# A hybrid decoder layer on one core: weight sums and stores one step later, accumulators loaded ahead, operand jobs on three tiles

## The chip, the cores and the metric

The kernel runs on one core of one Trainium2 chip. The metric is the device time of one execution in microseconds (us), as the median of several runs. The engines are named as in the profile: PE (matmul, with its weight loads PEld), DVE, ACT, POOL, and SP, which here only issues DMAs. Each engine and each engine's DMA queue takes its instructions in a fixed order; an instruction that waits holds up all that stand behind it on the same engine.

## The reference

One layer with 1024 tokens and width 1024. The input is normalised, projected into three branches (M: mLSTM, D: differential attention, C: cross-attention into 256 memory tokens), and each branch's output y is projected again; a sigmoid gate from the same normalised input weighs each projection, and the sum goes through an output projection and back onto the residual. A squared-ReLU MLP of width 4096 follows.

```python
g_m, g_d, g_c = jnp.split(jax.nn.sigmoid(h @ w_gate[l] + b_gate[l]), N_BRANCH, axis=-1)
merged = g_m * (y_m @ w_proj_m[l]) + g_d * (y_d @ w_proj_d[l]) + g_c * (y_c @ w_proj_c[l])
x = x + merged @ w_out[l]
h2 = rms_norm(x, norm_mlp_g[l])
x = x + jnp.square(jax.nn.relu(h2 @ w_up[l])) @ w_down[l]
```

All is float32. A float32 operand is split into a rounded high part (ACT, a cast) and a remainder (DVE, a subtraction), and a product is made of three matmuls (`mm3`, L119).

## The kernel before

**The first part** (to 1250 us on the trace) makes the normalised input `hT`, runs branch C, branch M and branch D, and spreads the gate projections (`gate_steps`, L449, 12 groups of 32 steps, a step is one `mm3` of 3 matmuls) between them. Two runs of gate steps stand by themselves: 64 steps between branch M and branch D (L1672), and 96 steps after branch D (L1695). The branches leave their outputs in DRAM (`yd`), the gates theirs (`gdr`).

**Operand jobs.** The branch projections, the MLP's up and down projection use a scheme with 7 instead of 8 block products (`PROD`, L1123). It needs sums of operand blocks. For an operand x, four blocks are combined by four subtractions (`wino_t`, L1134: three on DVE, one on POOL). For the branch outputs this is done by jobs (`x_jobs`, L1141): a job loads blocks of y on SP, makes the sums, and stores the result to DRAM (`xtd`) on SP. The jobs are a generator that is stepped once for each gate step; `waits` says how many steps lie between load, sums, store and the next load. In the run ahead of branch D there are eight jobs of 512 columns (C 0 to 3, M 3 to 0) on two tiles, after branch D eight of 256 columns (D 0 to 3) on one tile.

**The stream** (`stream`, L1280, from 1252 us to the end) is a row of steps n = 0 to 187: 48 for the branches in the order C, M, D (12 runs of four steps), 12 for the output projection, 64 for the up projection U (16 runs of four, u = 0 to 15), 64 for the down projection N (16 passes p of four). A step of a branch, of U or of N is 21 matmuls of 128x512 into seven PSUM banks (bank names rotate over eight); at the end of a run `sums` (L1335) combines the seven banks on ACT and DVE, and the next run takes over the banks as they come free.

Beside the matmuls of step n stand, in program order, `side(n)` (L1304): first the weight split for step n + 3, then a list `todo[n]` of other work, which `at(n, ...)` fills.

- *Weights.* `self.raws` lists raw weights, mostly in pairs (two steps' worth). `w_load` (L1194) issues a pair's two DMAs on SP into one of two buffers (`wrs`) and right behind them the pair's four sums on POOL (`wino_s`, L1127). `w_split` (L1213) splits one step's weights into one of three buffers (`wos`) with ACT and DVE, and when it has split the last of a pair it calls `w_load` for the next pair that uses that buffer.
- *Operands.* `x_load` (L1232) loads an x operand into one of the slots of `SLOT` on SP, `x_split` (L1248) splits it with ACT and DVE. A slot comes free when PE has used the operand that it held. For M and D, operand 0 is loaded at step 5 and 21, and 1 to 3 at 12 to 14 and 28 to 30. `x_direct` (L1255) makes a U operand from SBUF, with `wino_t`.
- *Gates.* `fetch` (L1309) loads a gate's tiles on SP, `gate` (L1314) multiplies on DVE and adds on POOL, `operands` (L1327) splits the merged sum for the output projection.
- *U's results.* `use_up` (L1491) scales a run's four results and squares them, and stores three blocks to `rd` from ACT's queue; `up_rest` (L1500) makes the four sums with `wino_t` and stores them on SP, at step 64 + 4u (u = 15 at 126). N's operands are loaded from `rd`.
- *Accumulators.* N has four groups g of seven accumulators in SBUF. In the first pass of each group (p = g) four of them are loaded with the residual (`x1d`) on SP when the pass's matmuls are traced, then the banks are added (DVE) or copied (ACT). The accumulators take over the memory of the pools that `accum` closes at step 126, among them the two tiles of `use_up` and `up_rest`.

**What sets the order.** Calls through `self.V`, `self.G`, `self.S`, and in the stream `self.A`, are pinned (`InOrder`, L57): each is kept behind the instruction that was traced just before it on its engine. Calls through `nc.vector`, `nc.sync` and the like are not pinned; the framework places them by its own estimate. Gate steps and their stores, and the sums of jobs, are of this kind; loads and stores of jobs are pinned.

Of the kernel before, what the change touches and what calls it, by code (L numbers as in the profile page):

```python
# [71 lines left out]
class Layer:  # L72
# [1068 lines left out]
    def x_jobs(self, pool, jobs, n, waits):  # L1141

        nc = self.nc
        for s, kp in jobs:
            for c in range(0, 512, n):
                r = pool.tile([P, 4, n], F32, tag="xj", name=self.name("xj"))
                for k in range(2):
                    src = self.yd[self.YOF[s]][2 * kp + k].rearrange("p (h n) -> p h n", h=2)
                    self.S.dma_start(r[:, 2 * k : 2 * k + 2], src[:, :, c : c + n])
                for _ in range(waits[0]):  # L1150
                    yield
                self.wino_t(r, r, nc.vector, nc.gpsimd)
                for _ in range(waits[1]):
                    yield
                self.S.dma_start(self.xtd[s][kp][:, :, c : c + n], r)
                for _ in range(waits[2]):
                    yield

    def s_open(self):
# [31 lines left out]
        self.X, self.W, self.wraw, self.nraw = {}, {}, {}, 0  # L1191
        return right

    def w_load(self):  # L1194
# [12 lines left out]
        else:  # L1207
            for i, s in enumerate(srcs):
                self.S.dma_start(r[:, i, 0:4], s)
            self.wino_s(r, self.G)  # L1210
            self.wraw[m] = [r[:, i] for i in range(2)]

    def w_split(self, m, split=None):  # L1213
# [10 lines left out]
        if i == len(self.wraw[j]) - 1:  # L1224
            self.w_load()

# [27 lines left out]

    def x_direct(self, s, kp, b):  # L1255
# [3 lines left out]
        self.wino_t(b, b, self.V, self.G)  # L1259
        self.split2(t[:, 0, 3:7], t[:, 1, 3:7], b)  # L1260

    def s_early(self):

        self.x_load("C", 0)
        self.w_load()
        yield
        self.x_load("C", 1)
        self.w_load()
        for _ in range(20):
            yield  # L1270
        for kp in range(2):
            for i in range(2):
                self.x_split("C", kp, (i,), self.split)
                for _ in range(10):
                    yield
        for kp in range(2):
            self.w_split(kp, self.split)
            yield

    def stream(self):  # L1280
# [23 lines left out]
        def side(n):  # L1304
            self.w_split(n + 3)
# [73 lines left out]
        self.w_split(2)  # L1379
# [23 lines left out]
        self.w_split(n + 3)  # L1403
# [41 lines left out]
        for g in range(4):  # L1445
# [12 lines left out]
            if g == 3:  # L1458
# [4 lines left out]
                self.w_split(n + 3)  # L1463
# [36 lines left out]
        def up_rest(u):  # L1500
            t = T["o"].tile([P, 4, 512], F32, tag="o", name=self.name("xts"))
            self.wino_t(T["b"], t, V, G)
            S.dma_start(self.rd[u, :, 3:7], t)

        for u in range(16):
            at(126 if u == 15 else 64 + 4 * u + (u == 0), up_rest, u)
# [16 lines left out]

        at(126, accum)
        for u in range(16):
# [3 lines left out]
            self.w_split(n + 3)  # L1529
# [20 lines left out]

# [225 lines left out]
```

## Time and profile before

| | us |
|---|---|
| median of three runs | 2334.99 |
| the runs | 2328.87 to 2336.34 |
| the profiled execution | 2336.45 |
| its span, first to last instruction | 2334.7 |

| engine | busy us of the span | share |
|---|---|---|
| PE | 2171.2 | 93% |
| DVE | 1493.0 | 64% |
| ACT | 1022.1 | 44% |
| POOL | 591.6 | 25% |

The mean granted TensorE clock is 0.969. Times on the trace count from the span's start. In a trace row, `out<-in` gives the tiles by their names in the program: `xj` is a job's tile, `xo` an operand x, `wraw` raw weights, `wo` split weights, `p` a PSUM bank, `u` and `c` results of `sums`, `gl` a gate's tile, `mg` the merged sum, `rq` and `xts` the tiles of `use_up` and `up_rest`, `acc` an accumulator, `dsg`, `dq`, `dk`, `dv` tiles of branch D, `y`, `gates`, `r_d`, `x_d` and `xtC_d` tensors in DRAM. L67 is the line of the pinning helper, so that many rows have that line. A row of SPq is the issue of DMAs, not their transfer.

### The profile page before, as it was taken

The page shows a single profiled execution, that of the slowest core. Times are in us where ns is not written, and L with a number is a line of the kernel's source. Part 1 is how long each engine was busy: PE and PEld are TensorE (multiplying, and loading weights), DVE is VectorE, ACT ScalarE, POOL GpSimd, SP SyncE. Part 2 cuts the span into 40 slices and gives each one's busy share as a digit, 9 for nine tenths or more (in the row PEclk, how much of TensorE's full clock was granted, in tenths as well). Part 3 has the DMA queues.
Part 4 walks back from the last instruction along what each step waited for, and adds up shares of the span by engine and source line. Part 5 has one row for each costly group of instructions (what it writes and reads, how often), then busy time and mean ns, then how long its engine had stood idle before and what let it go on. Part 6 is the DMA issues. An engine that isn't in the chain of part 4 may idle for free.

```text
span 2334.7 us, 30365 instructions
## 1 busy us (share of the span) xinstructions
PE 2171.2 (93%) x10953; PEld 1852.5 (79%) x10953; DVE 1493.0 (64%) x2732; ACT 1022.1 (44%) x1991; POOL 591.6 (25%) x564
## 2 busy tenths in 40 slices
PE   7999999999969999999996998899899997679999
PEld 5788888888869999999875776787688876568887
DVE  6643566553337777777532878874677776446789
ACT  6543445443226666666531333233344444323333
POOL 2100000000111111111011446623444443234542
PEclk9999999999979999999998999999999998789999
DMA  6023222212853333333365455233244445444444
GB/s 237 28 93 107 64 69 77 70 49 72 287 162 88 91 91 91 89 84 80 90 215 178 148 203 198 86 122 131 92 139 152 155 166 212 165 136 148 150 149 162
DMA packets 127676, 299.26 MB, mean 128 GB/s; under 512 B 13569, under 2 KB 30246, under 8 KB 120486
## 3 DMA queue, kind: packets, MB, share of 16 engines
q1 hardware_dynamic: 125222, 284.75, 38.2%
q10 hardware_dynamic: 2304, 12.58, 1.3%
q8 instruction: 86, 1.41, 0.3%
q14 instruction: 64, 0.52, 0.1%
HBM read 196.58 MB, written 75.53 MB: 117 GB/s over the span
## 4 chain that ended last, share of the span: by engine, by line
PE 66%; DMA 11%; DVE 10%; ACT 4%; issue 4%; POOL 3%; SPq 2%; DVEq 0%; POOLq 0%; ACTq 0%
PE mm L93 29%; PE p L93 25%; PE sc L93 5%; DMA xj<-y 4%; PE po L93 3%; DVE wo L67 2%; PE tp L96 2%; SPq L67 1%; POOL wraw L67 1%; DVE u L67 1%; DVE gl L67 1%; DMA acc<-x_d 1%; ACT xo L67 1%; DMA y<-yd 1%; DMA gl<-gates 1%
## 5 line engine op out<-in xcount | busy, mean ns | idle before, releaser
L93 PE MATMUL p<-xo,wo 128*128 128x512 f32 x3696 | 884.1, 401 | 97.1 <-DVE acc L67 24.7
L93 PEld LDWEIGHTS p<-xo,wo 128*128 128x128 f32 x3696 | 709.9, 193 | 270.0 <-DVE acc L67 26.4
L93 PE MATMUL mm<-w,hT 128*128 128x384 f32 (+3 forms) x2496 | 477.4, 334 | 33.9 <-DVE dsg L114 26.3
L67 POOL TENSOR_TENSOR wraw<-wraw 128x256 f32<-128x256 f32 x352 | 370.9, 1064 | 538.8 <-DMA wraw<-in_wdown 198.2
L93 PE MATMUL mm<-hT,w 128*128 128x512 f32 x1920 | 465.9, 395 | 3.1 <-ACT gt L473 3.1
L93 PEld LDWEIGHTS mm<-w,hT 128*128 128x128 f32 x2496 | 392.8, 191 | 48.3 <-issue 21.4
L93 PEld LDWEIGHTS mm<-hT,w 128*128 128x128 f32 x1920 | 353.3, 188 | 77.7 <-ACT gt L473 4.0
L67 ACT CAST wo<-wraw 128x896 fp32r<-128x896 f32 (+1 forms) x186 | 172.4, 932 | 455.3 <-PE p L93 277.1
L67 DVE TENSOR_TENSOR wo<-wraw,wo 128x896 fp32r<-128x896 f32 (+1 forms) x186 | 231.4, 1250 | 149.3 <-ACT wo L67 148.8
L114 DVE TENSOR_TENSOR w<-raw,w 128x256 fp32r<-128x256 f32 (+3 forms) x272 | 129.1, 497 | 58.9 <-ACT w L113 58.3
L113 ACT CAST w<-raw 128x256 fp32r<-128x256 f32 (+3 forms) x272 | 121.0, 469 | 67.6 <-PE mm L93 25.0
L1009 ACT ACTIVATE dpe<-sc,dst,drr 128x256 f32<-128x256 f32 (+7 forms) x128 | 106.7, 834 | 100.0 <-DVE dst L1005 92.6
L67 DVE TENSOR_TENSOR xo<-xo 128x1536 fp32r<-128x1536 f32 (+1 forms) x58 | 124.3, 2153 | 32.7 <-ACT xo L67 32.5
L67 ACT CAST xo<-xo 128x1536 fp32r<-128x1536 f32 (+1 forms) x58 | 97.3, 1691 | 47.3 <-DMA xo<-y 26.1
L129 POOL TENSOR_SCALAR hss<-hss 128x4 f32<-128x4 f32 x8 | 3.3, 411 | 414.6 <-ACT mscr L754 272.7
L1001 DVE CUSTOM_DVE_ANT_0 sc<-sc,tmask 128x256 f32<-128x256 f32 (+7 forms) x128 | 96.9, 757 | 12.6 <-PE sc L93 12.6
L67 DVE TENSOR_TENSOR u<-u,p 128x512 f32<-128x512 f32 x140 | 93.7, 686 | 12.0 <-PE p L93 0.5
L93 PE MATMUL sc<-dk,dq 128*128 128x512 f32 (+3 forms) x384 | 90.4, 343 | 0.0
L129 POOL TENSOR_SCALAR drr<-drr 128x16 f32<-128x16 f32 x16 | 3.3, 206 | 304.1 <-DVE drr L955 304.1
L93 PE MATMUL po<-mh,wo 128*128 128x512 f32 x256 | 78.9, 389 | 0.0
L473 ACT ACTIVATE gt<-mm,dv 128x512 f32<-128x512 f32 x48 | 32.9, 688 | 103.3 <-PE mm L93 55.0
L93 PE MATMUL po<-dv,daT 128*128 128x256 f32 x576 | 75.4, 274 | 0.6 <-DVE daT L114 0.6
(268 smaller groups left out, 2474.6 us busy)
## 6 DMA issues: line engine op xcount, KB each, us to landing
xo<-r_d SPq DMA_DIRECT2D x19, 1024.0 KB, 9.2
dk<-dsg SPq DMA_DIRECT2D x64, 256.0 KB, 4.0
wraw<-in_wup SPq DMA_DIRECT2D x64, 256.0 KB, 4.2
r_d<-xts SPq DMA_DIRECT2D x16, 1024.0 KB, 4.9
wraw<-in_wdown SPq DMA_DIRECT2D x64, 256.0 KB, 3.1
xo<-r_d SPq DMA_DIRECT2D x19, 768.0 KB, 7.2
raw<-in_wgate SPq DMA_DIRECT2D x48, 256.0 KB, 3.2
gates<-gt SPq DMA_DIRECT2D x48, 256.0 KB, 3.3
```

What stands on the lines that cost most here:

```text
L67: return self.tc.keep_in_program_order(f(*a, **k))
L93: self.pin(self.nc.tensor.matmul(out, l, r, start=start, stop=stop))
L96: self.pin(self.nc.tensor.transpose(out, x, self.ident))
L113: nc.scalar.copy(hi, src)
L114: nc.vector.tensor_sub(lo, src, f32(hi))
L129: g.tensor_scalar(r, ss, 1.0 / width, EPS, op0=ALU.mult, op1=ALU.add)
L473: nc.scalar.activation(t, ps, AF.Tanh, bias=self.bg[:, ft : ft + 1], scale=0.5)
L1001: V.tensor_tensor_reduce(out=sc[:, 0:n], in0=sc[:, 0:n], in1=self.tmask[:, D - n : D], scale=1.0, scalar=-3.0e38, op0=ALU.add, op1=ALU.max ...
L1009: nc.scalar.activation(pe[c][:, 0:n], sc[:, 0:n], AF.Exp, bias=t8[:, 2 + c : 3 + c], scale=rr[:, i, c : c + 1], accum_out=t8[:, 4 + c : 5 ...
```

## The change

Weights: `w_load` issues only the DMAs; the sums of a loaded pair are made by `w_sums`, which the new `w_next` calls at the next step. `w_next` takes the place of `w_split` in the stream: sums of what was loaded at the step before, loads for the buffers that came free at the step before, then the split. U's stores of sums move one step later (`up_store`). The accumulators of group g are loaded at step 126, 129, 133 and 137 by `acc_load`. `x_direct` makes all four sums on DVE (`x_fold`). Jobs: all have 256 columns and three tiles, a job's load is issued ahead of the sums and the store of the job before it. The run ahead of branch D has C 2, C 3 and M 0 (six jobs), the run after it C 0 and C 1, M 1 to 3 and D 0 to 3 (18 jobs); C 0 and C 1 are not stored but split straight into the operand's slot, so that `s_early` no longer loads and splits them. `s_early` also loads a third pair of weights.

```diff
--- before.py
+++ after.py
@@ -1138,23 +1138,34 @@
         V.tensor_sub(t[:, 2], b[:, 2], t[:, 1])
         V.tensor_sub(t[:, 3], b[:, 3], t[:, 2])
 
-    def x_jobs(self, pool, jobs, n, waits):
-
-        nc = self.nc
-        for s, kp in jobs:
-            for c in range(0, 512, n):
-                r = pool.tile([P, 4, n], F32, tag="xj", name=self.name("xj"))
+    def x_jobs(self, pool, jobs, wait):
+
+        V, G = self.nc.vector, self.nc.gpsimd
+        items = [(s, kp, slice(c, c + 256)) for s, kp in jobs for c in (0, 256)]
+        tiles = []
+        for i in range(len(items) + 1):
+            if i < len(items):
+                s, kp, c = items[i]
+                r = pool.tile([P, 4, 256], F32, tag="xj", name=self.name("xj"))
                 for k in range(2):
                     src = self.yd[self.YOF[s]][2 * kp + k].rearrange("p (h n) -> p h n", h=2)
-                    self.S.dma_start(r[:, 2 * k : 2 * k + 2], src[:, :, c : c + n])
-                for _ in range(waits[0]):
-                    yield
-                self.wino_t(r, r, nc.vector, nc.gpsimd)
-                for _ in range(waits[1]):
-                    yield
-                self.S.dma_start(self.xtd[s][kp][:, :, c : c + n], r)
-                for _ in range(waits[2]):
-                    yield
+                    self.S.dma_start(r[:, 2 * k : 2 * k + 2], src[:, :, c])
+                tiles.append(r)
+            for _ in range(wait[0]):
+                yield
+            if i:
+                s, kp, c = items[i - 1]
+                r = tiles.pop(0)
+                x = self.X[s, kp] if s == "C" and kp < 2 else None
+                if x is not None:
+                    self.split(x[:, 0, 0:3, c], x[:, 1, 0:3, c], r[:, 1:4])
+                self.wino_t(r, r, V, G)
+            for _ in range(wait[1]):
+                yield
+            if i and x is not None:
+                self.split(x[:, 0, 3:7, c], x[:, 1, 3:7, c], r)
+            elif i:
+                self.S.dma_start(self.xtd[s][kp][:, :, c], r)
 
     def s_open(self):
 
@@ -1188,7 +1199,9 @@
         for p in range(16):
             for k in (p, p + 2):
                 item("w", a["wdown"][p % 4][:, k % 16], a["wdown"][p % 4][:, (k + 1) % 16])
-        self.X, self.W, self.wraw, self.nraw = {}, {}, {}, 0
+        self.X, self.W, self.wraw, self.nraw, self.freed, self.fresh = {}, {}, {}, 0, 0, []
+        for k in range(2):
+            self.x_tile("C", k)
         return right
 
     def w_load(self):
@@ -1207,8 +1220,14 @@
         else:
             for i, s in enumerate(srcs):
                 self.S.dma_start(r[:, i, 0:4], s)
+            self.fresh.append(r)
+            self.wraw[m] = [r[:, i] for i in range(2)]
+
+    def w_sums(self):
+
+        for r in self.fresh:
             self.wino_s(r, self.G)
-            self.wraw[m] = [r[:, i] for i in range(2)]
+        self.fresh = []
 
     def w_split(self, m, split=None):
 
@@ -1222,7 +1241,15 @@
         (split or self.split2)(t[:, 0], t[:, 1], r)
         self.W[m] = t
         if i == len(self.wraw[j]) - 1:
+            self.freed += 1
+
+    def w_next(self, m):
+
+        self.w_sums()
+        for _ in range(self.freed):
             self.w_load()
+        self.freed = 0
+        self.w_split(m)
 
     def x_tile(self, s, kp):
         slot = self.SLOT[s][kp % 4]
@@ -1252,30 +1279,37 @@
             c = (slice(0, 3), slice(3, 7))[i]
             (split or self.split2)(t[:, 0, c], t[:, 1, c], f32(t[:, 1, c]))
 
+    def x_fold(self, b, t, V):
+
+        V.tensor_sub(t[:, 1], b[:, 0], b[:, 1])
+        V.tensor_sub(t[:, 0], b[:, 2], b[:, 0])
+        V.tensor_sub(t[:, 2], b[:, 2], t[:, 1])
+        V.tensor_sub(t[:, 3], b[:, 3], t[:, 2])
+
     def x_direct(self, s, kp, b):
 
         t = self.x_tile(s, kp)
         self.split2(t[:, 0, 0:3], t[:, 1, 0:3], b[:, 1:4])
-        self.wino_t(b, b, self.V, self.G)
+        self.x_fold(b, b, self.V)
         self.split2(t[:, 0, 3:7], t[:, 1, 3:7], b)
 
     def s_early(self):
 
-        self.x_load("C", 0)
-        self.w_load()
-        yield
-        self.x_load("C", 1)
-        self.w_load()
+        for _ in range(2):
+            self.w_load()
         for _ in range(20):
             yield
-        for kp in range(2):
-            for i in range(2):
-                self.x_split("C", kp, (i,), self.split)
-                for _ in range(10):
-                    yield
+        self.w_sums()
+        for _ in range(60):
+            yield
         for kp in range(2):
             self.w_split(kp, self.split)
             yield
+        self.w_load()
+        self.freed = 0
+        for _ in range(15):
+            yield
+        self.w_sums()
 
     def stream(self):
 
@@ -1302,7 +1336,7 @@
         four = lambda: (new("c11"), new("c21"), new("u3", pairs), new("u2", pairs))
 
         def side(n):
-            self.w_split(n + 3)
+            self.w_next(n + 3)
             for f in todo.pop(n, []):
                 f()
 
@@ -1376,7 +1410,7 @@
         at(32, open_hi)
         self.x_load("C", 2)
         self.x_load("C", 3)
-        self.w_split(2)
+        self.w_next(2)
         self.x_split("C", 2)
         at(0, self.x_split, "C", 3)
         for r in range(12):
@@ -1400,7 +1434,7 @@
             todo.setdefault(m, []).insert(m > n + 1, lambda s=s, u=u: fetch(s, u, 0))
             todo.setdefault(m + 1, []).insert(0, lambda s=s, u=u, cs=cs: gate(s, u, cs, 0))
             side(n)
-        self.w_split(n + 3)
+        self.w_next(n + 3)
         extra.close()
         T["hj"] = R("mhj", his, 2)
         gate("D", 3, cs, 1)
@@ -1460,7 +1494,7 @@
                 held.close()
                 self.xs["F"], self.xs["G"] = R("xsF"), R("xsG")
                 dg = L("dgp").tile([P, NT, P], F32, name="dg")
-                self.w_split(n + 3)
+                self.w_next(n + 3)
                 self.x_direct("U", 3, T["b"])
             else:
                 side(n)
@@ -1500,10 +1534,15 @@
         def up_rest(u):
             t = T["o"].tile([P, 4, 512], F32, tag="o", name=self.name("xts"))
             self.wino_t(T["b"], t, V, G)
-            S.dma_start(self.rd[u, :, 3:7], t)
+            T["rd"] = self.rd[u, :, 3:7], t
+
+        def up_store():
+            S.dma_start(*T["rd"])
 
         for u in range(16):
-            at(126 if u == 15 else 64 + 4 * u + (u == 0), up_rest, u)
+            m = 126 if u == 15 else 64 + 4 * u + (u == 0)
+            at(m, up_rest, u)
+            at(m + (u < 15), up_store)
         at(110, self.x_load, "N", 0)
         at(113, self.x_split, "N", 0, (0,))
         at(114, self.x_split, "N", 0, (1,))
@@ -1521,12 +1560,18 @@
             lp = L("acc")
             accs.extend(lp.tile([P, 512], F32, name=f"acc{i}") for i in range(28))
 
+        def acc_load(g):
+            for j, f, hf in ((1, 0, 1), (6, 0, 0), (4, 1, 1), (5, 1, 0)):
+                S.dma_start(accs[7 * g + j], half(self.x1d, 2 * g + f, hf))
+
         at(126, accum)
+        for g in range(4):
+            at(126 + 4 * g - (g > 0), acc_load, g)
         for u in range(16):
             ps = run(12 + u, (0, 1, 2, 3), "U", n, mid)
             n += 4
             cs = sums(ps, four())
-            self.w_split(n + 3)
+            self.w_next(n + 3)
             if 0 < u < 15:
                 use_up(u, cs)
             else:
@@ -1547,9 +1592,6 @@
                     side(n)
             acc = accs[7 * g : 7 * g + 7]
             if new:
-
-                for j, f, hf in ((1, 0, 1), (6, 0, 0), (4, 1, 1), (5, 1, 0)):
-                    S.dma_start(acc[j], half(self.x1d, 2 * g + f, hf))
                 V.tensor_sub(acc[6], acc[6], acc[5])
             add = V.tensor_add
             o = lambda f, hf, t: S.dma_start(half(self.out, 2 * g + f, hf), t)
@@ -1669,8 +1711,8 @@
                     self.branch_m(T3(), gm, 1, gnext)
                 with tc.tile_pool(name="wpg", bufs=13, reuse_waits="tile") as self.wp, tc.tile_pool(name="rpg", bufs=3, reuse_waits="tile") as self.rp:
                     self.gwp, self.grp = self.wp, self.rp
-                    with tc.tile_pool(name="pg", bufs=2) as self.gpool, tc.tile_pool(name="xj", bufs=2) as xj:
-                        jobs = self.x_jobs(xj, [("C", k) for k in range(4)] + [("M", k) for k in (3, 2, 1, 0)], 512, (5, 3, 0))
+                    with tc.tile_pool(name="pg", bufs=2) as self.gpool, tc.tile_pool(name="xj", bufs=3) as xj:
+                        jobs = self.x_jobs(xj, [("C", 2), ("C", 3), ("M", 0)], (4, 5))
                         for _ in range(2 * 32):
                             next(jobs, None)
                             next(self.gates)
@@ -1692,8 +1734,8 @@
                         self.gpool = T4()
                         self.branch_d(T4())
                     right = self.s_open()
-                    with tc.tile_pool(name="pgh", bufs=2) as self.gpool, tc.tile_pool(name="xjd", bufs=1) as xj:
-                        jobs = self.x_jobs(xj, [("D", k) for k in range(4)], 256, (5, 2, 4))
+                    with tc.tile_pool(name="pgh", bufs=2) as self.gpool, tc.tile_pool(name="xjd", bufs=3) as xj:
+                        jobs = self.x_jobs(xj, [("C", 0), ("C", 1)] + [(s, k) for s in "MD" for k in range(s == "M", 4)], (3, 4))
                         early = self.s_early()
                         for _ in self.gates:
                             next(early, None)
```

## The prediction

> **What bounds the kernel now.** I read the page first and then the table by windows, cut at the stages: window, its length, busy us (and instructions) of PE, its weight loads, DVE, ACT and POOL, then granted clock, DMA share, GB/s.
>
> ```profile
> span 2334.7 us, 30365 instructions
> ...
> 619.00:690.00 71.00, 45.40 (x236) 44.30 (x235) 25.58 (x64) 17.45 (x51) 11.59 (x9) 0.78 0.63 205
> 1181.00:1300.00 119.00, 95.83 (x408) 75.90 (x407) 47.30 (x62) 34.04 (x45) 24.14 (x25) 0.93 0.63 205
> 1300.00:1540.00 240.00, 219.24 (x912) 173.55 (x911) 199.59 (x191) 79.36 (x83) 136.76 (x109) 0.96 0.48 160
> 1540.00:1680.00 140.00, 127.33 (x541) 103.11 (x540) 77.66 (x89) 51.75 (x69) 44.58 (x40) 0.94 0.31 101
> 1680.00:1920.00 240.00, 240.00 (x1049) 196.47 (x1048) 179.97 (x223) 113.84 (x165) 108.10 (x111) 1.00 0.45 156
> 1920.00:2120.00 200.00, 151.47 (x585) 119.34 (x584) 105.23 (x108) 69.84 (x80) 63.51 (x62) 0.85 0.47 165
> ```
>
> TensorE is the bound and in the U stage has no gap, so a better order can win nothing there. Its gaps lie in five stretches: 25.6, 23.2, 20.8, 12.7 and 48.5 us (length less PE busy), where the clock is below 1 too. I call them A to E. The table of waits (engine, what it waited for, us in total, times, longest) names two causes in C and E:
>
> ```profile
> PE p L93 <- DVE acc L67: 24.7, 4, 9.1
> PE p L93 <- ACT u L67: 21.6, 3, 13.0
> ```
>
> The rest is the timeline: start, length, engine, instruction, and in brackets the engine's idle time before it and its releaser. **One cause returns: a DMA or a POOL operation stands in its queue behind one that waits for something unrelated.** One nearly undisturbed run of four steps gives the rate, 19.33/84 = 0.230 us a matmul, 4.8 us a step of 21:
>
> ```profile
> 1509.06 19.33 PE L93 MATMUL p<-xo,wo 128*128 128x512 f32 x84 [0.25 <-DVE wo L67]
> ```
>
> **The change part by part**, in us of the profiled execution, which took 2336.45 (span 2334.7 and 1.75 around it), 1.46 above the median of the runs, 2334.99.
>
> **A, the gate run ahead of branch D, and D's start.**
>
> ```profile
> 619.40 8.51 PE L93 MATMUL mm<-w,hT 128*128 128x384 f32 x48
> ...
> 632.37 13.85 PE L93 MATMUL mm<-w,hT 128*128 128x384 f32 x63 [4.46 <-DVE dv L114]
> ...
> 647.42 0.75 DVE L117 SCALAR_TENSOR_TENSOR dsg<-pr,dv,dsg 128x512 fp32r<-128x512 f32 x1 [2.35 <-ACT dsg L116]
> ...
> 668.53 2.48 SPq L884 DMA_DIRECT2D dq<-dsg  x4
> ...
> 674.26 8.73 PE L93 MATMUL mm<-w,hT 128*128 128x384 f32 x36 [21.14 <-DVE dsg L114]
> ```
>
> Eight jobs go one by one here, because SP reaches the next load only after it has waited for this job's sums and issued its store; they outlast the gates. Branch D's dq load, whose data are ready at 648.2, leaves SP at 668.5, 20.3 late, and PE stands for 21.14. The change leaves six half-size jobs (12 loads, 6 stores), traced within 63 of the 64 gate steps, each stored one job later. So the queue is free when branch D comes: of 21.14 I leave 1.5 (issue and landing of dq), the 4.46 (late weights) goes, and 36 matmuls at the full clock take 36 x 8.51/48 = 6.4, not 8.73. Gain 19.6 + 4.5 + 2.3 = **26** (18 if 8 of the wait stays, 29 if nothing does).
>
> **B, the last gate run and the first four stream steps.** It takes over what left A: 18 half-size jobs in place of 8 (36 loads; 14 stores, since C 0 and 1 are split in SBUF and their six reloads go).
>
> ```profile
> 1181.89 17.97 PE L93 MATMUL mm<-hT,w 128*128 128x512 f32 x78
> ...
> 1209.65 2.00 SPq L67 DMA_DIRECT2D xj<-y  x2
> ...
> 1270.94 1.18 SPq L67 DMA_DIRECT2D xj<-y  x2
> ...
> 1279.65 0.47 SPq L67 DMA_DIRECT2D xo<-xtC_d  x1
> ...
> 1291.67 43.13 PE L93 MATMUL p<-xo,wo 128*128 128x512 f32 x188 [1.76 <-DVE xo L67]
> ...
> xj<-y SPq DMA_DIRECT2D x16, 256.0 KB, 4.1
> ```
>
> With one tile a job takes (1270.94 - 1209.65)/6 = 10.2. C 2 and 3 are loaded among them; the fourth stream step starts at 1291.67 and ends 4.8 later, at 1296.5, which is 16.9 after C 3's last load was issued. With three tiles a job's path is the load's issue 1.2, its landing 4.1, and for sums and store an estimated 2.5: 7.8, two at a time 3.9. The program gives a job seven gate steps, 7 x 3 x 0.230 = 4.8. The 96 gate steps last 66, to 1248, and hold fourteen jobs; five turns remain, and C 2 is now chained behind them all on SP: 1248 + 5 x 4.8 = 1272, or 1268 at 3.9. C 3's last load follows 3 later and the fourth step ends at 1272 + 3 + 16.9 = 1292, at worst 1293.5. Gain **3** (from -56 at 7.8 a job, 1184 + 19 x 7.8 + 20 = 1352, to +8). This is the weak spot: most of B's 23.2 does not go, it becomes a gap behind the jobs' tail.
>
> **C, branches M and D of the stream.**
>
> ```profile
> 1340.65 2.37 DVE L67 SCALAR_TENSOR_TENSOR mg<-gl,c 128x512 f32<-128x512 f32 x2
> ...
> 1345.23 0.81 SPq L67 DMA_DIRECT2D wraw<-in_wpm  x2
> ...
> 1346.62 0.84 SPq L67 DMA_DIRECT2D xo<-y  x2
> ...
> 1361.44 8.88 PE L93 MATMUL p<-xo,wo 128*128 128x512 f32 x30 [0.79 <-DVE c L67]
> ...
> 1464.73 7.19 POOL L67 TENSOR_TENSOR wraw<-wraw 128x256 f32<-128x256 f32 x4 [10.03 <-DMA wraw<-in_wpd]
> ...
> 1476.37 11.81 PE L93 MATMUL p<-xo,wo 128*128 128x512 f32 x38 [4.85 <-DVE c L67]
> ```
>
> Operand M 1 is loaded at 1346.6 because the weight load ahead of it waits till 1345.2 for its buffer's split; ACT then waits for M 1 with the copy of a finished bank behind it, and PE for ACT: 4.3, a fifth of the row of 21.6. Issued a step later, that weight load is out of the way, and SP waits only for the ring tile that the gate at 1340.65 frees, about 1342. M 1 comes 4.2 earlier. DVE's splits, next in line, leave 1.8 of 4.3 + 0.79: 3.3 won, and 2.0 of clock (30 matmuls need 6.9, not 8.88). Branch D's operands repeat the pattern: 10.6 for both. At 1464.73 POOL has waited 10 for a weight DMA, the gate's sums behind it and DVE behind those. With the weights' sums one step later the gate's go first: the 4.85 goes, and 1.5 of the 3.1 that 38 matmuls lost (8.7 against 11.81). Gain 10.6 + 6.4 = **17** (5 if POOL only changes which work is late, 22).
>
> What hides the later weight sums: the pair loaded at one step is split two steps on and multiplied two after that, 19 us, against 4.1 to land, up to 7.2 for sums, an estimated 2.6 for the split. Without that cover each us beyond costs PE one. Queued behind a late sum are POOL's next gate or store sums, behind a late split ACT's bank copies. I cost it at nothing in the full stretches.
>
> **D, output projection into U.**
>
> ```profile
> 1608.46 2.48 DVE L67 SCALAR_TENSOR_TENSOR x<-po,x 128x512 f32<-128x512 f32 x4 [6.60 <-DMA x<-in_xT]
> ...
> 1623.92 1.29 POOL L67 TENSOR_TENSOR h<-h 128x512 f32<-128x512 f32 x1
> ...
> 1629.53 1.22 PE L93 MATMUL p<-xo,wo 128*128 128x512 f32 x2 [4.07 <-ACT wo L67]
> ...
> 1632.02 13.50 PE L93 MATMUL p<-xo,wo 128*128 128x512 f32 x52 [1.26 <-DVE wo L67]
> ```
>
> Two delays feed these gaps: the load of x behind a weight load on SP, and x_direct's POOL subtraction behind weight sums. The first gets the queue, the second moves to DVE, 2.48/4 = 0.6 by the row above in place of 1.29, beside PE's work (DVE is busy 78 of 140 here). I take 8 of the stretch's 12.7, and 2 of clock (52 matmuls need 12.0, not 13.50, and the next gap costs some): gain **10** (4 to 14).
>
> **E, U into the down projection.**
>
> ```profile
> 1962.39 0.33 SPq L67 DMA_DIRECT2D r_d<-xts  x1
> ...
> 1974.25 1.65 PE L93 MATMUL p<-xo,wo 128*128 128x512 f32 x3 [12.96 <-ACT u L67]
> ...
> 2008.44 0.33 SPq L67 DMA_DIRECT2D r_d<-xts  x1
> ...
> 2019.14 21.60 PE L93 MATMUL p<-xo,wo 128*128 128x512 f32 x84 [9.09 <-DVE acc L67]
> ...
> 2045.38 22.10 PE L93 MATMUL p<-xo,wo 128*128 128x512 f32 x84 [4.64 <-DVE acc L67]
> ...
> 2073.18 21.89 PE L93 MATMUL p<-xo,wo 128*128 128x512 f32 x84 [5.69 <-DVE acc L67]
> ...
> 2100.37 19.88 PE L93 MATMUL p<-xo,wo 128*128 128x512 f32 x75 [5.30 <-DVE acc L67]
> ```
>
> The store of U's tile 14 leaves at 1962.4, its POOL part having stood behind weight sums; N 1's load waits behind the store, ACT's split for N 1, PE for ACT: 12.96. With the store a step later N 1 is loaded when its slot frees, three steps before U's end (1961.3 - 14.4 = 1947): I leave 4, gain 9, and 2 of clock. Accumulators of groups 1 to 3 now load two steps ahead: 4.64 + 5.69 + 5.30 = 15.6 falls to 2.0, gain 13.6, and their slow clock, 22.10 + 21.89 - 2 x 19.33 and 19.88 - 17.25, gives 8.0. Group 0 still follows tile 15's store, whose memory it takes; POOL no longer waits for a pair's DMA there, I put the store 5.4 earlier: 5.4 of 9.09. Sum 9 + 2 + 13.6 + 8.0 + 5.4 = **38** (26 if N 1 still comes late, 52 if group 0's wait goes whole).
>
> [...]
>
> **Sum:** 26 + 3 + 17 + 10 + 38 = 94; 2336.45 - 94 = **2242.5**.
>
> **Rivals.** *R1, the tail of B:* a job takes 6, between 4.8 and 7.8, because DMA is shared with gates, weights and stores. C 2 leaves at 1184 + 19 x 6 = 1298, the fourth step ends 20 later, 21.5 after today's: 2242.5 + 3 + 21.5 = **2267**. For it: landing alone is 4.1, and gate stores stand in the same queue; against: three tiles, so no load waits for a store's landing.
> *R2, DVE and POOL in each other's way:* POOL no longer idles behind DMAs, so its sums run beside DVE's splits, and C is where DVE has least to spare (200 busy of 240). A split's mean is 1261 ns, yet one beside POOL's gate sums took 2.17:
>
> ```profile
> 1410.98 2.17 DVE L67 TENSOR_TENSOR wo<-wraw,wo 128x896 fp32r<-128x896 f32 x1
> ...
> L67 DVE TENSOR_TENSOR wo<-wraw,wo 128x896 fp32r<-128x896 f32 x174 | 218.4, 1261 | 133.6 <-ACT wo L67 133.1
> ```
>
> Then C's 17 go: **2259.5**. Against it: POOL has no more work than before. [...]
> *R3, the change does not do what it says:* only some DMAs and sums are pinned to the one traced before, the rest float, and waits on SP and POOL persist in A and E: half of 64 is lost, **2274.5**. For it: today C 2's load leaves among jobs traced before it.
> *R4, slower:* the tiles do not overlap and a job costs 10.2 as now: 1184 + 19 x 10.2 + 20 = 1398, 101 late, **2347**. It decides from 9.7 a job, where B eats the other 91. Against: every load precedes the store that it waited for.
>
> **How the numbers follow.** Forecast 0.67, R1 0.13, R2 0.08, R3 0.07, R4 0.05. 0.3% (7) is about what a measurement can tell from no change. All but R4 are faster by far; 0.01 of R4 may land within, and 0.01 for two losses at once. The range: all low ends in A, C, D and E with R1's -21.5 give 31.5, unlikely together; I take 42, **2294**, which holds R1 to R3. All high ends give 29 + 8 + 22 + 14 + 52 = 125, **2211**. B's -56 alone gives 2301 and stays outside, with R4.
>
> **What would show it.** A: no PE gap over 3, dq leaving within 2 of its data. B: one gap of 12 to 20 before the third stream step, its load chained behind jobs. C: PE's waits for ACT u under 2 each. D: no POOL h. E: PE waiting for DVE acc long once only, and no load behind an r_d store. Wrong: new waits of PE for wo in the U stage, or a job's period over 6.

## The result and the profile after

The changed kernel takes **2259.7 us** (2256.11 to 2261.07), the kernel before it on the same chip 2331.93 (2328.75 to 2336.34): a ratio of 0.9687, interval 0.9663 to 0.971. The forecast was 2242.5. The profiled execution took 2260.53.

To see where it went, both traces were cut at the same places of the program: branch D's first score matmul ends A; the first of ACT's copies u<-p ends B, the 12th C, the 14th D, the 27th the rest of the U stage (U); E is the 28th copy (N1, the down projection's start), the first accumulator instruction of its second pass (group 0) and of its fifth (groups 1 to 3); the end counts from the 14th pass. Between the fifth pass and the 14th, and ahead of A, both kernels take the same time to within 0.2.

| Stage | before, us | after, us | gained | forecast |
|---|---|---|---|---|
| A (from branch M's last transposes) | 106.8 | 77.1 | 29.8 | 26 |
| B | 608.0 | 607.5 | 0.5 | 3 |
| C | 244.7 | 243.4 | 1.3 | 17 |
| D | 149.3 | 137.9 | 11.4 | 10 |
| U | 252.6 | 253.4 | -0.8 | 0 |
| E: N1 | 36.1 | 22.4 | 13.7 | 11 |
| E: group 0 | 61.9 | 58.9 | 3.0 | 5.4 |
| E: groups 1 to 3 | 82.8 | 58.3 | 24.6 | 21.6 |
| end | 45.0 | 52.5 | -7.5 | 0 |

The table of windows of the changed kernel, cut at the same work as before (window, length, then busy us and instructions of PE, its weight loads, DVE, ACT, POOL, then clock, DMA share, GB/s):

```profile
619.00:661.00 42.00, 41.47 (x241) 40.35 (x240) 15.71 (x50) 15.83 (x46) 6.59 (x4) 1.00 0.47 132
1151.00:1269.00 118.00, 97.58 (x408) 77.93 (x407) 62.02 (x97) 35.11 (x50) 33.72 (x37) 0.90 0.75 249
1269.00:1508.00 239.00, 218.66 (x908) 172.16 (x908) 202.57 (x189) 78.62 (x83) 142.54 (x107) 0.96 0.46 160
1508.00:1638.00 130.00, 124.49 (x549) 102.31 (x548) 83.00 (x94) 53.14 (x72) 42.23 (x36) 0.97 0.33 108
...
1878.00:2036.00 158.00, 138.99 (x580) 111.02 (x579) 107.51 (x107) 69.66 (x80) 65.24 (x60) 0.95 0.55 201
2036.00:2258.00 222.00, 214.42 (x932) 176.35 (x930) 163.42 (x179) 75.36 (x65) 84.12 (x82) 0.98 0.42 149
```

A's gap of 25.6 is 0.5 now, D's 12.7 is 5.5, E's 48.5 is 19.0. B's 23.2 is 20.4, and C's 20.8 is 20.3. The last stretch has 7.6 of gaps; the same work before, in the same view, had 3.6:

```profile
2120.00:2334.00 214.00, 210.40 (x929) 173.86 (x927) 170.62 (x178) 75.48 (x65) 97.07 (x80) 1.00 0.44 155
```

The table of waits shows the exchange (engine, what it waited for, us in total, times, longest), of the changed kernel and, for two rows, of the kernel before:

```profile
ACT wo L67 <- POOL wraw L67: 162.2, 34, 9.2
...
PE p L93 <- DVE c L67: 15.9, 8, 3.4
PE p L93 <- DVE acc L67: 8.1, 1, 8.1
...
PE mm L93 <- DVE dsg L114: 5.5, 7, 0.9
...
PE p L93 <- ACT u L67: 2.5, 3, 1.5
```

```profile
ACT wo L67 <- POOL wraw L67: 123.1, 37, 6.2
...
PE p L93 <- DVE c L67: 10.2, 8, 4.8
```

PE's wait for ACT u fell from 21.6 to 2.5, for acc from 24.7 to 8.1, and of the 21.14 for dsg no more than 0.9 at a time is left; PE's wait for DVE c grew from 10.2 to 15.9. ACT waits 162.2 for POOL's weight sums, where it waited 123.1 before; 73.6 of this lie in C, where it was 42.2.

The timeline of A and B (start, length, engine, instruction, and in brackets the idle time before it and its releaser):

```profile
618.21 0.56 SPq L67 DMA_DIRECT2D xtM_d<-xj  x1
...
640.57 2.44 SPq L884 DMA_DIRECT2D dq<-dsg  x4
...
646.64 6.54 PE L93 MATMUL mm<-w,hT 128*128 128x384 f32 x36 [0.35 <-DVE dsg L114]
...
1220.12 1.35 SPq L67 DMA_DIRECT2D xj<-y  x2
...
1236.17 1.72 SPq L67 DMA_DIRECT2D xj<-y  x2
...
1246.20 0.79 PE L93 MATMUL p<-xo,wo 128*128 128x512 f32 x1 [15.04 <-ACT xo L67]
```

In A the last job's store leaves at 618, 22 ahead of dq, and of the 21.14 of PE's idle time 0.35 is left. In B five loads leave from 1220.12 to 1236.17, a job each 4.0, and one gap of 15.04 stands ahead of the third step, its operand behind the jobs.

C and the end need the experiments. In C the 4th of ACT's copies u<-p comes 6.6 earlier relative to the third, by the earlier operand; by the fifth, 5.2 of it are gone:

```profile
1318.00:1322.00 4.00, 4.00 (x19) 3.32 (x18) 3.71 (x3) 3.47 (x3) 2.87 (x2) 1.00 1.01 408
```

```profile
1321.41 15.74 SPq L67 DMA_DIRECT2D wraw<-in_wpm  x4
...
1331.48 7.61 POOL L67 TENSOR_TENSOR wraw<-wraw 128x256 f32<-128x256 f32 x4 [6.05 <-DMA wraw<-in_wpm]
...
1339.12 1.79 ACT L67 CAST wo<-wraw 128x896 fp32r<-128x896 f32 x2 [5.41 <-POOL wraw L67]
...
1341.16 1.62 DVE L67 TENSOR_TENSOR wo<-wraw,wo 128x896 fp32r<-128x896 f32 x1
...
1346.31 0.58 ACT L67 COPY u<-p 128x512 f32<-128x512 f32 x1 [5.40 <-DVE mg L67]
...
1346.95 0.96 PE L93 MATMUL p<-xo,wo 128*128 128x512 f32 x3 [1.48 <-ACT u L67]
```

The first fence is the table by windows, the second the timeline. DMA's share is 1.01 while the three operands come in, and a pair asked for from 1321.41 on is there at 1331.48, 10 later and not 4.1. Its sums take 7.61, ACT stands 5.41 for them, and DVE has split the first weight of the pair at 1342.78. But DVE did not stand for it: it goes over to this weight without a gap, straight from an operand's split. Between the two copies it is idle for 0.52 only. The table by windows, from the 4th copy to the 5th, first of the kernel before, then of the changed one:

```profile
1358.37:1378.58 20.21, 18.79 (x71) 14.86 (x72) 19.56 (x19) 10.62 (x10) 5.87 (x5) 0.83 0.52 193
```

```profile
1320.89:1346.31 25.42, 21.64 (x91) 16.09 (x89) 24.90 (x20) 10.62 (x11) 17.39 (x11) 1.00 0.44 166
```

In both kernels DVE is busy for all but some 0.6 of this run and makes the same instructions in the same order; POOL's busy time there grew from 5.87 to 17.39, and DVE's from 19.56 to 24.90. So DVE is late with the gate, ACT's copy of the finished bank waits 5.40 for the gate, and PE stands 1.48 for that copy. The run from the 8th copy to the 9th repeats it: 20.24 with 19.56 of DVE and 5.93 of POOL before, 25.39 with 24.84 and 15.95 now. The experiments show what lengthens DVE's instructions.

### The profile page after: what moved, and what is told of

It reads as the page before. It is cut to its first block, busy times and chain, and to the rows that moved or that the text cites. A ratio compares the mean times of both kernels' runs of the same rounds, so it can differ in the third digit from the quotient of the medians.

```text
span 2258.8 us, 30482 instructions
## 1 busy us (share of the span) xinstructions
PE 2156.7 (95%) x10953; PEld 1841.5 (82%) x10953; DVE 1516.9 (67%) x2764; ACT 1021.1 (45%) x1995; POOL 591.1 (26%) x568
## 5 line engine op out<-in xcount | busy, mean ns | idle before, releaser
L93 PE MATMUL p<-xo,wo 128*128 128x512 f32 x3696 | 873.8, 398 | 63.4 <-ACT xo L67 22.2
L93 PE MATMUL mm<-w,hT 128*128 128x384 f32 (+3 forms) x2496 | 472.2, 331 | 8.9 <-DVE dsg L114 5.5
L93 PEld LDWEIGHTS mm<-hT,w 128*128 128x128 f32 x1920 | 353.2, 188 | 77.1 <-ACT gt L473 2.4
L93 PEld LDWEIGHTS mm<-w,hT 128*128 128x128 f32 x2496 | 388.2, 189 | 22.8 <-DVE dsg L114 7.7
L67 DVE TENSOR_TENSOR xo<-xo 128x1536 fp32r<-128x1536 f32 (+1 forms) x58 | 127.1, 2207 | 20.8 <-ACT xo L67 19.8
L67 ACT CAST xo<-xo 128x1536 fp32r<-128x1536 f32 (+1 forms) x58 | 97.0, 1691 | 25.7 <-DMA xo<-y 21.4
L1001 DVE CUSTOM_DVE_ANT_0 sc<-sc,tmask 128x256 f32<-128x256 f32 (+7 forms) x128 | 97.1, 758 | 12.7 <-PE sc L93 12.6
L67 DVE TENSOR_TENSOR u<-u,p 128x512 f32<-128x512 f32 x140 | 93.8, 686 | 12.7 <-DVE c L67 0.9
L93 PEld LDWEIGHTS po<-dv,daT 128*128 128x128 f32 x576 | 74.0, 189 | 1.6 <-DVE daT L114 0.9
```

The source lines that it names most:

```text
L67: return self.tc.keep_in_program_order(f(*a, **k))
L93: self.pin(self.nc.tensor.matmul(out, l, r, start=start, stop=stop))
L1001: V.tensor_tensor_reduce(out=sc[:, 0:n], in0=sc[:, 0:n], in1=self.tmask[:, D - n : D], scale=1.0, scalar=-3.0e38, op0=ALU.add, op1=ALU.max ...
```

## The experiments

Each run is named by its label. All differ from the changed kernel by the edit shown. "C" below is the stage of the table in the profiled execution; the changed kernel was profiled twice and had C at 243.4 and 246.0, so under 3 there tells nothing. Up to 3.8 us came and went ahead of A, in code that no kernel changes.

**The parts apart: e_jobs, e_w_old, e_w_only.** e_jobs keeps only the new jobs. e_w_old keeps all but the later weight step:

```
     def w_next(self, m):
-        self.w_sums()
+        self.w_split(m)
         for _ in range(self.freed):
             self.w_load()
         self.freed = 0
-        self.w_split(m)
+        self.w_sums()
```

e_w_only keeps the jobs and the later weight step, and puts these back, the accumulators' load into the pass that uses it (e_jobs too, beside the edit above):

```
-            at(m + (u < 15), up_store)
+            at(m, up_store)
 ...
-            at(126 + 4 * g - (g > 0), acc_load, g)
 ...
+                acc_load(g)
 ...
-        self.x_fold(b, b, self.V)
+        self.wino_t(b, b, self.V, self.G)
```

> The new branch operands' jobs alone; weight steps, accumulator loads, the store of U's tiles and x_direct's sums stand as before. Theory (the parts A and B of the gain come from the jobs and from nothing else): branch D's start 29 to 30 us earlier, the first stream step 31 earlier, nothing more behind it: 2331.9 - 31 = 2301 (2297 to 2305). Rival (the jobs need the later weight steps to fit): the stream starts 10 to 20 earlier, 2312 to 2322.

> The changed kernel with the weight steps' load and sums back in the step of the split that frees the buffer; all else as changed. Theory (the later weight step gives back in branches M and D what the earlier operand loads win there, and loses 7.5 at the end because the last pairs' loads stand behind the output's stores): M and D within 3 of the changed kernel, the end 5 to 8 better, U into N up to 5 worse: 2251 to 2259. Rival (the later weight step carries the gain from U into the down projection): that gap returns, 13 worse there, 2263 to 2268.

> The jobs and the later weight steps; accumulator loads, the store of U's tiles and x_direct's sums as before. Theory (the parts add up: later weights alone carry about half of what the gap before the second operand of the down projection won, some 4 of the accumulators' 24, 3 of the output projection's 11, nothing in branches M and D, and lose 7.5 at the end): 7 us less than the kernel with the jobs alone, a ratio of 0.985 to 0.987. Rival (they need each other: without the later store and loads the later weights win nothing there): a ratio of 0.989 to 0.992.

Measured: e_jobs 2310.97 (ratio 0.9885, 0.9863 to 0.9906), e_w_old 2276.6 (0.9742, 0.9717 to 0.9767), e_w_only 2312.86 (0.9904, 0.9889 to 0.9918). By stage, gained against the kernel before:

| Kernel | A | B | C | D | U | N1 | group 0 | groups 1-3 | end |
|---|---|---|---|---|---|---|---|---|---|
| changed | 29.8 | 0.5 | 1.3 | 11.4 | -0.8 | 13.7 | 3.0 | 24.6 | -7.5 |
| e_jobs | 29.0 | -2.3 | -1.3 | 2.1 | -0.7 | -1.2 | -0.9 | -1.1 | -0.1 |
| e_w_only | 29.6 | -1.7 | -0.8 | 12.2 | -38.2 | 0.9 | 5.1 | 24.1 | -7.0 |
| e_w_old | 29.1 | -0.4 | 1.4 | 7.7 | -0.3 | 6.9 | -3.1 | 20.1 | -0.5 |

A is the jobs' alone. e_jobs gained less than expected, as B gave 2 back. My theory of e_w_old was right on C and on the end, and wrong on the rest; the time lies above its range and its rival's too, since without the later weight step 20.6 are lost from D to E (51.9 against 31.3). And the theory of e_w_only, that the parts add up, falls. Its total lies in the rival's range by chance: the later weights do win in D and in the groups, and lose it in U. In D and in groups 1 to 3 they **stand in for each other**: the later weights alone give 12.2 and 24.1, the other edits alone 7.7 and 20.1, both together about as much. Why shows on SP, in the timelines of e_jobs and of e_w_only in the same pass:

```profile
2039.55 1.01 SPq L67 DMA_DIRECT2D wraw<-in_wdown  x2
2040.60 1.85 SPq L67 DMA_DIRECT2D acc<-x_d  x4
...
2048.66 21.98 PE L93 MATMUL p<-xo,wo 128*128 128x512 f32 x84 [5.56 <-DVE acc L67]
```

```profile
2016.02 94.23 PE L93 MATMUL p<-xo,wo 128*128 128x512 f32 x405 [8.94 <-DVE acc L67]
...
2043.06 0.86 SPq L67 DMA_DIRECT2D wraw<-in_wdown  x2
2043.97 1.91 SPq L67 DMA_DIRECT2D acc<-x_d  x4
```

In e_jobs the accumulators' load leaves at 2040.60, 2.7 after the pass's first copy into an accumulator (2037.9), and PE stands 5.56. In e_w_only it leaves at 2043.97, 7.3 ahead of that copy (2051.3), and PE runs 405 matmuls on. Its place in the code is the same in both, and a weight load leaves right ahead of it in both; but in e_jobs that one waits for the split of the same step (to 2039.55), in e_w_only for the split of the step before (to 2043.06).

For N1 they **need each other** (6.9 and 0.9 alone, 13.7 together), and in U the later weights do harm by themselves: 37.5 more than e_jobs. e_w_only there, in the timeline:

```profile
1737.81 0.33 SPq L67 DMA_DIRECT2D r_d<-xts  x1
1738.31 2.89 SPq L67 DMA_DIRECT2D wraw<-in_wup  x4
...
1747.90 0.94 ACT L67 CAST wo<-wraw 128x896 fp32r<-128x896 f32 x1 [11.04 <-POOL wraw L67]
...
1757.24 0.73 PE L93 MATMUL p<-xo,wo 128*128 128x512 f32 x2 [2.16 <-ACT wo L67]
```

Without the moved store a weight load stands on SP behind the store of U's tile, which waits for POOL and DVE; two pairs then leave at once, ACT waits 11.04 and PE for ACT. From 1650 to 1940 ACT waits 13 times for POOL's weight sums, 126.5 in all, and PE 8 times for ACT, 14.3.

**What gives C's gain back: order on the queues? e_load_now, e_load_end.** e_load_now loads the weights in the step of the split and leaves only the sums a step later; e_load_end loads at the end of that step, behind its operand loads.

```
     def w_next(self, m):
         self.w_sums()
+        self.w_split(m)
         for _ in range(self.freed):
             self.w_load()
         self.freed = 0
-        self.w_split(m)
```

(e_load_end: the loop of loads becomes w_more(), which each step calls after its todo list.)

> The changed kernel with the weight load issued in the step of the split, and only its sums one step later. Theory (POOL's weight sums stand behind the gate's sums of the same run and hold up ACT and DVE): the sums now come a step earlier, ahead of the gate's; ACT's waits for wraw in M and D fall from 8.7 and 9.2 to under 4, the operand 1 loads are late again, M and D win 0 to 8; the end wins 5 to 8: 2245 to 2255. Rival (DVE and POOL in each other's way): M and D as in the changed kernel, only the end wins: 2252 to 2255, and DVE's pairs of splits in M and D still take over 5.

> The changed kernel with the weight load at the end of the step of the split, behind that step's operand loads, and its sums one step later, ahead of the gate's. Theory (order on POOL): operand 1 early and weight sums ahead of the gate's: M and D win 8 to 17, the end 5 to 8: 2236 to 2247. Rival (DVE and POOL in each other's way): M and D as in the changed kernel, the end alone wins: 2252 to 2255.

Measured: e_load_now 2272.78 (0.9723, 0.9702 to 0.9744), e_load_end 2261.45 (0.9672, 0.9652 to 0.9693). C was 244.1 and 242.4: **the theory of POOL's order falls**. e_load_end decides it, since the sums now stand ahead of the gate's, the 4th copy comes as early as in the changed kernel, and C stayed. e_load_now missed its range because N1 won 6.8 of 13.7 (the weight load stood ahead of N1's load again) and groups 1 to 3 19.5. The end lost 0.1 in the first and 5.7 in the second, where I had expected it to win back 5 to 8 of its 7.5.

**POOL's sums left out, or idle ones in their place: e_nosum, e_dummy, e_dummy6.** In e_nosum the weights of branches M and D have no sums on POOL, and an ACT copy fills the planes; e_dummy and e_dummy6 have the same, and eight or six additions on POOL that nobody waits for (the range is 8, 6, and no loop in e_nosum; pair[j] is the pair's tile).

```
     def w_sums(self):
         for r in self.fresh:
+            if 9 <= self.nraw <= 24:
+                for _ in range(8):
+                    self.G.tensor_add(self.tmaskT, r[:, 1, 0], r[:, 1, 3])
+                continue
             self.wino_s(r, self.G)
 ...
     def w_split(self, m, split=None):
 ...
+        if 9 <= j + 1 <= 24 and i == 0:
+            q = self.pair[j]
+            self.A.copy(q[:, :, 4:7], q[:, :, 0:3])
```

> The changed kernel; for the weights of the stream's branches M and D the four sums of each pair are left out on POOL, and one copy on ACT (of three planes over the three that the sums would fill) stands ahead of the split, so these products differ from the reference. Both theories: branches M and D win what POOL's sums cost them, 8 to 17 of the 17 forecast: 2243 to 2252. A third (DMA is full there, and late weights hold everything up): under 4, 2256 to 2260.

> As the kernel without POOL's weight sums in branches M and D (the same sums left out, the same copy on ACT), but POOL makes eight additions of 128x128 on each of those pairs into a tile that nobody reads, where the sums stood: the load on POOL and on SBUF stays, and nobody waits for it. Theory 1 (order: ACT waits for POOL's late sums): M and D win as much as without the sums, 8 to 17. Theory 2 (DVE's instructions are stretched beside POOL's): M and D win less than half of what leaving the sums out wins, and pairs of DVE's splits still take over 4.5.

> As the kernel whose POOL makes eight idle additions for each pair of M and D (same sums left out, same copy on ACT), with six, so that POOL is busy as long as with the sums themselves (6 x 0.82 against 4 x 1.19). From the first sum step of the stream to the twelfth the changed kernel took 243.4, without sums 221.5, with eight idle additions 233.0. Theory (both causes, and the stretching goes with POOL's busy time): 229 to 232, a ratio of 0.961 to 0.963. Rival (POOL beside DVE costs nothing that depends on its length): 233 or more, 0.9638.

Measured: e_nosum 2241.27 (0.9588, 0.9573 to 0.9602), C 221.5; e_dummy 2253.36 (0.9638, 0.9624 to 0.9652), C 233.0; e_dummy6 2250.94 (0.9636, 0.962 to 0.9652), C 230.4. So POOL's weight sums cost C 22 of 243.4 in the changed kernel, more than the 8 to 17 expected. The third theory falls: the pair of the run shown above lands as late in e_nosum (the four weight DMAs around this run take 5.4 in the median in both kernels, 1318 to 1346 and 1322 to 1346; the pair's own two take 8.5 in the changed kernel), and the run takes 20.22 all the same, as before the change. With idle work on POOL 10 (eight additions) to 13 (six, which keep POOL busy about as long as the sums, 15.42 between the 4th copy and the 5th against 17.39) of the 22 are still won. Neither theory alone was right; e_dummy6 has its C in the theory's range and its ratio just above it, by the rival's. How the 22 divide into waiting for the sums and DVE's lengthening is not to be read off these numbers, because the idle additions lengthen DVE's instructions less than the sums do (mg took 944 ns with six of them, 1224 with the sums). The run from the 4th copy to the 5th in e_nosum, then in e_dummy6:

```profile
1325.05:1345.27 20.22, 18.77 (x81) 14.39 (x80) 19.65 (x20) 12.20 (x13) 0.00 (x0) 1.00 0.48 181
```

```profile
1325.45:1347.67 22.22, 20.64 (x89) 15.92 (x88) 21.65 (x20) 12.20 (x12) 15.42 (x14) 1.00 0.52 196
```

DVE is idle for 0.6 in both and for 0.5 in the changed kernel (24.90 of 25.42), so here the whole difference is the length of DVE's instructions. From the 8th copy to the 9th it is the same: 25.39 in the changed kernel, 23.50 in e_dummy6, 20.25 in e_nosum, each with 0.6 of idle DVE. These two runs make 10.3 of the 22; how much of the other 12 is waiting stays open. The changed kernel's second profile shows that waiting has a part: its run from the 4th copy takes 25.78 with 23.66 of DVE, and DVE waits 1.6 of it for ACT's cast of late weights. The groups of DVE's instructions (busy us, then mean ns) in the run that begins with the 4th copy: the changed kernel, 1318 to 1346; e_nosum, 1322 to 1346; e_dummy6, 1323 to 1348:

```profile
L67 DVE TENSOR_TENSOR xo<-xo 128x2048 fp32r<-128x2048 f32 x3 | 8.5, 2826 | 0.0
...
L67 DVE TENSOR_TENSOR u<-u,p 128x512 f32<-128x512 f32 x5 | 3.4, 687 | 0.4
L67 DVE SCALAR_TENSOR_TENSOR mg<-gl,c 128x512 f32<-128x512 f32 x2 | 2.4, 1224 | 0.0
```

```profile
L67 DVE TENSOR_TENSOR xo<-xo 128x2048 fp32r<-128x2048 f32 x3 | 6.9, 2287 | 0.0
...
L67 DVE TENSOR_TENSOR u<-u,p 128x512 f32<-128x512 f32 x5 | 3.4, 687 | 0.4
...
L67 DVE SCALAR_TENSOR_TENSOR mg<-gl,c 128x512 f32<-128x512 f32 x2 | 1.3, 684 | 0.0
```

```profile
L67 DVE TENSOR_TENSOR xo<-xo 128x2048 fp32r<-128x2048 f32 x3 | 7.2, 2415 | 0.1
...
L67 DVE SCALAR_TENSOR_TENSOR mg<-gl,c 128x512 f32<-128x512 f32 x2 | 1.8, 944 | 0.0
```

The instructions with both inputs in SBUF are longer in the changed kernel, with POOL busy for 17.39 between the two copies, than in e_nosum, with POOL idle there (mg 1224 against 684, an operand's split 2826 against 2287); u<-u,p, with one input in PSUM, is 687 in both. In the kernel before, with POOL busy for 5.87 of 20.21 in this run, mg takes 684 and the split 2286.

**The end: e_end, e_best, e_best_again, e_changed_again.** e_end puts the weight load back into the step of the split, from the seventh pass of the down projection on (m is the weight that is split; the expectations call this pass the sixth); e_best does so in e_load_end.

```
         self.w_split(m)
+        if m > 150:
+            for _ in range(self.freed):
+                self.w_load()
+            self.freed = 0
```

> The changed kernel, but from the down projection's sixth pass on a weight pair is loaded in the step of the split that frees its buffer, as before. Theory (the end's loss of 7.5 is the last pair standing on SP behind the operand's load and the output's stores): passes up to the 12th as in the changed kernel, the end 5 to 8 better, 0.9687 x 2331.9 less 7, a ratio of 0.966. Rival (the loss comes from the stores or DVE and not from where the weight load stands): no difference.

> The weight load at the end of its step, behind that step's operand loads, its sums one step later, and from the down projection's sixth pass on in the step of the split. Theory (this takes the 5 us that the former kernel with the load at the end of the step lost in its last passes, and keeps the rest): 5 us less than that kernel, a ratio of 0.965 to 0.9665. Rival (the loss only moves to another pass): 0.967 to 0.969.

> The kernel with the weight load at the end of its step, and in the step of the split from the sixth pass of the down projection on, beside the changed kernel on one chip: 6 to 9 us less than the changed kernel (theory: the end's 7 and 1 of branches M and D), at least 3 if only the end wins in part.

> The changed kernel as it is, beside the kernel before it on one chip: a ratio of 0.966 to 0.971, as measured.

Measured: e_end 2257.58 (0.9655, 0.9639 to 0.9671), e_best 2254.85 (0.9647, 0.9633 to 0.9661). The end takes 45.5 in both, 52.5 in the changed kernel; the loss is where the load stands. The changed kernel's timeline, then e_end's:

```profile
2219.93 0.89 SPq L67 DMA_DIRECT2D xo<-r_d  x2
2220.93 1.07 SPq L67 DMA_DIRECT2D wraw<-in_wdown  x2
...
2229.91 3.07 POOL L67 TENSOR_TENSOR wraw<-wraw 128x256 f32<-128x256 f32 x4 [14.49 <-DMA wraw<-in_wdown]
2233.01 1.78 ACT L67 CAST wo<-wraw 128x896 fp32r<-128x896 f32 x2 [8.79 <-POOL wraw L67]
...
2242.52 11.71 PE L93 MATMUL p<-xo,wo 128*128 128x512 f32 x38 [3.22 <-DVE xo L67]
```

```profile
2194.71 60.73 PE L93 MATMUL p<-xo,wo 128*128 128x512 f32 x267
...
2220.60 6.25 SPq L67 DMA_DIRECT2D out<-acc  x4
...
2227.55 0.81 SPq L67 DMA_DIRECT2D wraw<-in_wdown  x2
...
2228.46 0.86 SPq L67 DMA_DIRECT2D xo<-r_d  x2
...
2231.29 4.73 POOL L67 TENSOR_TENSOR wraw<-wraw 128x256 f32<-128x256 f32 x4 [6.08 <-DMA wraw<-in_wdown]
```

In both the last pair leaves behind stores of the output. In the changed kernel it also leaves behind the last operand's load (2219.93), its sums begin 9 later (2229.91), and the lateness runs through POOL, ACT and DVE to PE (3.22). In e_end it leaves ahead of that load (2228.46), its sums begin 3.7 later, and PE has no gap in 267 matmuls. Counted from the 14th pass's first accumulator instruction (2206.22 and 2214.71) the sums begin 23.7 and 16.6 in, 7.1 apart. On one chip: e_best_again 2255.2 (0.9653, 0.9639 to 0.9668), e_changed_again 2264.52 (0.9695, 0.9681 to 0.971), 9.3 between them (6 to 9 expected), 6.9 of it at the end. This version beats both kernels.

## Why the prediction was right or wrong

The sign and the size held, the sum was 94 and 75.9 were won (spans). The differences, from the first table: A +3.8, B -2.5, C -15.7, D +1.4, U -0.8, E +3.3, end -7.5, together -18.0.

- **A, right, the gain 3.8 low.** I left 1.5 for dq's issue and landing and got 0.35, and e_jobs shows that nothing else carries it.
- **B, right in mechanism, a little high.** One gap ahead of the third step (15.04, 12 to 20 forecast), a job each 4.0 (3.9 to 4.8). R1 and R4 needed 6 and 9.7. The gain of 3 was a small difference of large numbers and came to between -2.3 and 0.6 in the runs.
- **C, wrong, and below my low end of 5.** The step that failed is the price of nothing for POOL's sums beside DVE: I let "DVE's splits, next in line," keep their old lengths and set against R2 that "POOL has no more work than before". The two gains are there: operand 1 leaves earlier, and the runs that end with the 4th and the 8th copy are 6.6 and 5.8 shorter. POOL's work in C did stay about the same (busy 142 of it before, 148 now). But it moved into the two runs that follow, where DVE splits operands and had some 0.6 to spare, and each of them grew by 5.2, 10.4 of the 15.7 that C fell short. "What hides the later weight sums" failed too: the landing took 10 and not 4.1, the sums 7.61, and the first split was done 21.4 after the issue, against a cover of 19. In the run shown DVE had no time to wait for it; what it cost in the rest of C stays open. That C is not to be had by order alone is shown by e_load_end (242.4), and that POOL's sums carry it by e_nosum. My sign for C came true (PE's waits for ACT u, 1.5 at most), so it told nothing.
- **R2** named C as the place and DVE beside POOL as the cause, and forecast 2259.5. Its mechanism is shown, with the same instructions of DVE at two lengths in the two runs above. Its total agrees by chance: it knew nothing of the end's 7.5 and B's 2.5, which cancel what A, C, D and E won beyond it. In the rows above mg takes 1224 ns against 684, and u<-u,p, with one input in PSUM, 687 in both.
- **D and E, right in size, partly wrong in cause.** I credited groups 1 to 3 to the accumulators' earlier loads and D to the x load and x_direct. Either these or the later weights carry all or most of it (24.1 or 20.1; 12.2 or 7.7). N1 needs both the store and the weight load out of its way; I had put the store and the weight sums ahead of it, not the weight load. Group 0 stayed behind tile 15's store, 3.0 won where I put 5.4. The high end of 52 is not what its condition gives: group 0's whole wait adds 3.7 to the 38, 6 with its clock (its 84 matmuls took 21.60 in the kernel before, against 19.33 in the nearly undisturbed run at 1509.06).
- **"I cost it at nothing in the full stretches"** held in U, but only because the store moved too (e_w_only: -38.2), which I did not see; and it failed at the end, where it cost 7.5.
- **R3** falls: dq, N1 and the accumulators' loads leave where the program puts them.

What stays open is how much of C the late weights cost beside DVE's lengthening, and whether they would still be late if they were loaded earlier; no kernel with an earlier load or a third weight buffer was tried.

## What to carry to other kernels

A transfer that is moved later on a queue must be followed past every store and load that now stands ahead of it, in each stage: the same move was worth 24 in one stage, needed a second edit in another (or cost 37) and lost 7.5 in a third. Cover that is worked out with a typical landing time has to be checked where the transfers come together, for there a pair took 10 to come in and not 4. And before one engine's work is moved beside another's, see what the other has to spare: DVE had 0.65 of 20.21 us where the weight sums came to lie, its instructions grew by 5.3 and the run by 5.2, nearly all that the earlier operand had won.

## What the runs showed of the hardware

In the run that begins with the 4th copy, DVE's instructions with two SBUF inputs were longer where POOL worked: mg took 684 ns with no weight sums on POOL, 944 with six idle additions of 128x128 for a pair, 1224 with the four sums of 128x256, and an operand's split 2287, 2415 and 2826. u<-u,p, with one input in PSUM, took 687, 686 and 687. One and the same row of DVE instructions, between the 4th copy and the 5th, took 19.56 us with POOL busy for 5.87 and 24.90 with POOL busy for 17.39. POOL's sums were longer beside DVE too: four additions of 128x256 took 3.07 us at 2229.91, where DVE stood idle from 2230.53 to 2233.99, and 7.61 at 1331.48, beside DVE's splits.
